# More first-half products before the second half is ready: fifteen tiles instead of ten between output projection and feed-forward

## The chip, the cores and the metric

The kernel runs on one core of one Trainium2 chip. The metric is the device time of one execution in microseconds (us), the median of several runs. The engines are TensorE (PE, with its weight loads PEld), VectorE (DVE), ScalarE (ACT), GpSimd (POOL) and SyncE (SP), which only issues transfers here.

## The reference, cut to what matters

One transformer layer over 640 tokens (128 context, 512 latent) of width 2048. The change lies between these lines:

```
o = concatenate([a, cm, pm], axis=-1) @ w_out
x = x + g1 * rmsnorm(o, g_post_mix)
h = rmsnorm(x, g_pre_ffn) * (1 + sc2) + sh2
gt, up = split(h @ w_ffn_in, 2, axis=-1)       # 2048 x 11264
f = (silu(gt) * up) @ w_ffn_out
x = x + g2 * rmsnorm(f, g_post_ffn)
```

`rmsnorm(x, g)` is `x * rsqrt(mean(x*x) + 1e-6) * g`, the mean being over the 2048 channels of a token.

## The kernel before

Everything is kept transposed: channels on the 128 partitions, tokens along the free dimension, and the 640 tokens are worked on as two halves of 320. Every fp32 operand of a product is split into a high and a low part (`hl`, `X`, `act`), and a product is three matmuls of 128x128 weights on 128x320 tokens (high-high, high-low, low-high, lines 1165 to 1167).

**Output projection.** It runs in two passes, one for each token half. While pass two runs, `chain()` normalises the first half: post-norm, residual, pre-norm, modulation, and the split into `X[1]` and `X[2]`. So when pass two ends, the first half is ready for the feed-forward, and the second is not.

**Feed-forward, first matrix.** There are 44 tiles (`FT`). For each, a 2x2 scheme with seven products (`PROD`, j = 0 to 6) replaces eight. Each product is two granules (z = 0, 1) of 12 matmuls: 14 granules in a tile, 616 in all, 7392 matmuls. Products j = 0 and j = 4 need `X[1]` and `X[2]` alone, that is the first token half; the other five need combinations with the second half (`X[3]` to `X[7]`). For the first `NEARLY` = 10 tiles ("early tiles") products 0 and 4 are done ahead, while the second half is still being normalised; their results `p1` and `f1` are put into DRAM (`ed`) and fetched again by `load_early` when the tile gets its other five products (10 granules, order 1, 2, 3, 6, 5). Tiles 10 to 43 follow, with all seven ("full tiles").

**The stream.** `Stream` S3 issues the granules in a fixed order. `S3.step()` fetches weights (SP queue, five buffers `ra` of 512 KB), splits the granule that is three ahead (`prep`: ACT writes the high part, line 1121, DVE the low part, line 1122), makes the weight sums five ahead (`make`: POOL, lines 1147 and 1150; j = 3 on DVE), issues 12 matmuls into a PSUM bank, and then the evacuations `after()` of the granule before. All engines take their instructions in the order of issue.

**The transition.** `chain2()` does the second half's post-norm and residual, and sums the squares for the pre-norm: DVE multiplies by the norm factor (line 992) and adds x (line 993), ACT squares (line 1001), POOL adds the eight squares into one (line 1004), TensorE sums over partitions with a matrix of ones (line 1009). `prep_steps()` multiplies by the second factor `y2` (line 1320), modulates (ACT, line 1325), forms the combinations of both halves (POOL and DVE, line 1147) and splits them into `X[3]` to `X[7]` (lines 1153 and 1154). Both are generators: between their steps the lists `FILB`, `FILL` and `FILP` say how many S3 steps are issued, 1 + 12 + 29 = 42 granules by the end of the preparation. After that comes the rest of the stream, and with it `mod5()`, the last modulation vector, computed on DVE (lines 1388 and 1390) in one small step after every third granule.

**Memory.** Eight PSUM banks of tag `u` rotate among the products. `p1` and `f1` have four buffers each (`NPF`).

## Time and profile before

| what | value |
|---|---|
| median of 3 runs | 2737.97 us (2735.94 to 2738.11) |
| the profiled execution | 2736.24 us, span 2734.5 us |
| TensorE busy | 2611.9 us (96%) of the span |
| VectorE busy | 2027.8 us (74%) |
| ScalarE, GpSimd busy | 1192.6 us (44%), 681.9 us (25%) |
| end of the output projection's matmuls | about 979.2 us from the start of the span |
| first matmul of the feed-forward's second matrix | 2124.89 us |

The span runs from the first to the last instruction of the profiled execution. All times in the rows are microseconds from its start; a busy TensorE is counted by its matmul records, which overlap. "PEclk" is the granted TensorE clock as a share of 2.4 GHz.

### The profile page before, as it was taken

The page shows a single profiled execution, that of the slowest core. Times are in us where ns is not written, and L with a number is a line of the kernel's source. Part 1 is how long each engine was busy: PE and PEld are TensorE (multiplying, and loading weights), DVE is VectorE, ACT ScalarE, POOL GpSimd, SP SyncE. Part 2 cuts the span into 40 slices and gives each one's busy share as a digit, 9 for nine tenths or more (in the row PEclk, how much of TensorE's full clock was granted, in tenths as well). Part 3 has the DMA queues.
Part 4 walks back from the last instruction along what each step waited for, and adds up shares of the span by engine and source line. Part 5 has one row for each costly group of instructions (what it writes and reads, how often), then busy time and mean ns, then how long its engine had stood idle before and what let it go on. Part 6 is the DMA issues. An engine that isn't in the chain of part 4 may idle for free.

```text
span 2734.5 us, 48244 instructions
## 1 busy us (share of the span) xinstructions
PE 2611.9 (96%) x18874; PEld 2515.4 (92%) x18874; DVE 2027.8 (74%) x3248; ACT 1192.6 (44%) x2427; POOL 681.9 (25%) x572
## 2 busy tenths in 40 slices
PE   5999999999899988999999999999999899999996
PEld 4898998899899987999999999999999899999985
DVE  5558874443545779777888888888786899999966
ACT  4232333333554646333333333333333655555554
POOL 2300020000112435544333333333333111111112
PEclk9999999999999999999999999999999999999998
DMA  8856565653445774443333333333332433333343
GB/s 310 297 187 220 197 195 199 221 189 123 159 147 168 212 250 145 147 160 125 128 107 120 124 117 111 127 125 107 121 124 81 140 107 121 110 120 106 98 130 109
DMA packets 182708, 415.88 MB, mean 152 GB/s; under 512 B 17872, under 2 KB 99920, under 8 KB 181968
## 3 DMA queue, kind: packets, MB, share of 16 engines
q1 hardware_dynamic: 151568, 316.58, 35.2%
q10 hardware_dynamic: 27296, 82.33, 9.5%
q0 software_dynamic: 3616, 13.90, 1.4%
q8 instruction: 148, 2.42, 0.4%
q14 instruction: 80, 0.66, 0.1%
HBM read 373.01 MB, written 39.71 MB: 151 GB/s over the span
## 4 chain that ended last, share of the span: by engine, by line
PE 66%; DVE 17%; ACT 5%; issue 5%; DMA 3%; POOL 2%; ACTq 1%; SPq 0%; DVEq 0%; POOLq 0%
PE pj L310 7%; PE pj L311 7%; PE pj L312 7%; PE u L1167 7%; PE u L1165 7%; PE u L1166 7%; DVE hl L1122 5%; PE bb L1165 3%; PE bb L1167 3%; PE bb L1166 3%; ACT hl L1121 2%; DVE f L1390 2%; PE bc L1165 2%; PE bc L1167 2%; PE bc L1166 2%
## 5 line engine op out<-in xcount | busy, mean ns | idle before, releaser
L1167 PE MATMUL u<-X,hl 128*128 128x320 f32 x2464 | 767.6, 312 | 23.7 <-DVE hl L1122 23.4
L1165 PE MATMUL u<-X,hl 128*128 128x320 f32 x2464 | 767.6, 312 | 8.2 <-ACT hl L1121 4.5
L1166 PE MATMUL u<-X,hl 128*128 128x320 f32 x2464 | 762.8, 310 | 0.0
L310 PE MATMUL pj<-act,hl 128*128 128x320 f32 x1664 | 525.1, 316 | 8.8 <-ACT act L250 4.7
L311 PE MATMUL pj<-act,hl 128*128 128x320 f32 x1664 | 516.0, 310 | 1.2 <-DVE act L150 0.7
L312 PE MATMUL pj<-act,hl 128*128 128x320 f32 x1664 | 515.4, 310 | 0.0
L1167 PEld LDWEIGHTS u<-X,hl 128*128 128x128 f32 x2464 | 464.2, 188 | 34.7 <-DVE hl L1122 34.5
L1165 PEld LDWEIGHTS u<-X,hl 128*128 128x128 f32 x2464 | 464.2, 188 | 15.8 <-ACT hl L1121 8.1
L1166 PEld LDWEIGHTS u<-X,hl 128*128 128x128 f32 x2464 | 464.3, 188 | 0.3 <-issue 0.2
L310 PEld LDWEIGHTS pj<-act,hl 128*128 128x128 f32 x1664 | 314.1, 189 | 33.8 <-issue 15.7
L150 DVE TENSOR_TENSOR hl<-ra,hl 128x512 fp32r<-128x512 f32 x244 | 183.5, 766 | 191.8 <-ACT hl L149 191.3
L311 PEld LDWEIGHTS pj<-act,hl 128*128 128x128 f32 x1664 | 314.2, 189 | 3.5 <-DVE act L150 2.1
L312 PEld LDWEIGHTS pj<-act,hl 128*128 128x128 f32 x1664 | 314.2, 189 | 0.2 <-DVE hl L150 0.2
L1122 DVE TENSOR_TENSOR hl<-ra,hl 128x512 fp32r<-128x512 f32 x264 | 244.0, 933 | 43.0 <-ACT hl L1121 42.5
L1150 POOL TENSOR_TENSOR s<-ra 128x512 f32<-128x512 f32 x88 | 145.0, 1647 | 335.0 <-DMA ra<-in_wfi 116.9
L1121 ACT ACTIVATE hl<-ra 128x512 fp32r<-128x512 f32 x264 | 159.4, 625 | 132.0 <-PE u L1167 106.0
L1121 ACT ACTIVATE hl<-s 128x512 fp32r<-128x512 f32 x176 | 110.2, 626 | 236.7 <-DVE s L1147 197.3
L1122 DVE TENSOR_TENSOR hl<-s,hl 128x512 fp32r<-128x512 f32 x176 | 133.4, 762 | 82.0 <-ACT hl L1121 80.9
L149 ACT ACTIVATE hl<-ra 128x512 fp32r<-128x512 f32 x244 | 148.2, 631 | 100.8 <-PE pj L312 56.9
L1122 DVE TENSOR_TENSOR hl<-sy,hl 128x512 fp32r<-128x512 f32 x176 | 139.2, 791 | 67.6 <-ACT hl L1121 67.2
L1147 POOL TENSOR_TENSOR sy<-ra,sy 128x512 f32<-128x512 f32 x88 | 133.7, 1519 | 151.4 <-DVE hl L1122 151.4
L1150 POOL TENSOR_TENSOR T<-T,raw 128x384 f32<-128x384 f32 (+1 forms) x56 | 54.8, 979 | 457.2 <-DVE T L1150 438.0
(343 smaller groups left out, 4926.3 us busy)
## 6 DMA issues: line engine op xcount, KB each, us to landing
ra<-in_wfi SPq DMA_DIRECT2D x196, 512.0 KB, 4.2
rb<-in_wada SPq DMA_DIRECT2D x96, 512.0 KB, 5.5
ra<-in_wada SPq DMA_DIRECT2D x64, 512.0 KB, 6.2
ra<-in_win ACTq DMA_DIRECT2D x56, 512.0 KB, 4.8
ra<-in_wout ACTq DMA_DIRECT2D x56, 512.0 KB, 4.1
raw<-in_wfo SPq DMA_DIRECT2D x48, 576.0 KB, 4.0
f<-in_wada SPq DMA_DIRECT2D x128, 128.0 KB, 2.1
fd<-f ACTq DMA_DIRECT2D x44, 320.0 KB, 2.2
```

Source lines behind the costliest of these rows:

```text
L149: act_e.activation(h, src, AF.Copy)
L150: dve.tensor_tensor(out=l, in0=src, in1=h.bitcast(F32), op=ALU.subtract)
L310: pe.matmul(ps, w[:, 0, k, :], rhs_h, start=start, stop=False)
L311: pe.matmul(ps, w[:, 0, k, :], rhs_l, start=False, stop=False)
L312: pe.matmul(ps, w[:, 1, k, :], rhs_h, start=False, stop=stop)
L1121: act_e.activation(g.hl[:, 0, :n], src, AF.Copy)
L1122: dve.tensor_tensor(out=g.hl[:, 1, :n], in0=src, in1=g.hl[:, 0, :n].bitcast(F32), op=ALU.subtract)
L1147: e.tensor_tensor(out=out, in0=a, in1=b, op=ALU.subtract)
L1150: e.tensor_tensor(out=out, in0=a, in1=b, op=ALU.add)
L1165: pe.matmul(ps, w[:, 0, j, :], xh, start=first and j == 0, stop=False, skip_group_check=True)
L1166: pe.matmul(ps, w[:, 0, j, :], xl, start=False, stop=False, skip_group_check=True)
L1167: pe.matmul(ps, w[:, 1, j, :], xh, start=False, stop=stop and j == n - 1, skip_group_check=True)
```

## The change

The early tiles become 15. `FILL` and `FILP` are rewritten (with `FILB` 1 + 18 + 44 = 63 granules by the end of the preparation). The tiles are then taken in the order 0, 15, 1, 16, ... 14, 29 and 30 to 43 (`ORDER3`), so an early tile alternates with a full one, and `mod5()` begins at once, a step after every fourth granule as long as early tiles are in the order, then after every third. In `chain2()` the squares are summed by TensorE alone: sixteen matmuls with the matrix of ones in place of seven POOL additions and two matmuls; DVE takes over the one block (i = 5) that POOL had. Both norm factors are written to PSUM banks (tags `y`, `s`), and six banks stay for `u`. The eight POOL subtractions for `X[7]` are issued between the splits in place of ahead of them. The weights of the feed-forward's first granules are fetched and split earlier, while the last output tile is projected. `p1` keeps three buffers and `f1` two; `mod5()` gets tiles of its own.

```
-        P2["y2"] = yst.enter_context(tc.tile_pool(name="yp", ...)).tile([P, TH], F32, tag="y2", name="y2")
...
-    def rsqrt_half(ps, y):
+    def rsqrt_half(ps, y, out=None):
...
-        rsqrt_to(y, v, t, ps[:, :TH], 1.0 / D)
-        return y
+        rsqrt_to(y, v, t, ps[:, :TH], 1.0 / D, out)
+        return y if out is None else out
...
-        y = rsqrt_half(ps, y_tile()).unsqueeze(1).to_broadcast([P, 2, TH])
+        y = rsqrt_half(ps, y_tile(), bank3("y", "y")).unsqueeze(1).to_broadcast([P, 2, TH])
         yield
         sq = {}
+        ps = bank3("xss", "s")
         for i in range(KP + 3):
             if i < KP:
-                e, t = (pool if i == 5 else dve), X["b", i]
-                e.tensor_tensor(out=t, in0=t, in1=y, op=ALU.mult)
-                e.tensor_tensor(out=t, in0=t, in1=x[i], op=ALU.add)
+                t = X["b", i]
+                dve.tensor_tensor(out=t, in0=t, in1=y, op=ALU.mult)
+                dve.tensor_tensor(out=t, in0=t, in1=x[i], op=ALU.add)
...
-            if k > 0:
-                pool.tensor_tensor(out=sq[0], in0=sq[0], in1=sq[k], op=ALU.add)
+            if k >= 0:
+                for z in range(2):
+                    pe.matmul(ps, ones, sq[k][:, z, :], start=k == 0 and z == 0, stop=k == KP - 1 and z == 1)
                 drop(sq[k])
             yield
-        ps = bank3("xss")
-        for z in range(2):
-            pe.matmul(ps, ones, sq[0][:, z, :], start=z == 0, stop=z == 1)
-        drop(sq[0])
-        rsqrt_half(ps, P2["y2"])
+        P2["y2"] = rsqrt_half(ps, y_tile(), bank3("y2", "y"))
...
-            if hf and n == KT - 1 and g == 1:
+            if hf and (n, g) == (KT - 2, 3):
                 x_item(lambda: S3.fetch())
+            if hf and (n, g) == (KT - 1, 2):
+                x_item(lambda: S3.prep(2))
...
-    def bank3(name="u"):
-        return P3["ps"].tile([P, 512], F32, tag="u", name=name)[:, :TH]
+    def bank3(name="u", tag="u"):
+        return P3["ps"].tile([P, 512], F32, tag=tag, bufs=6 if tag == "u" else 1, name=name)[:, :TH]
...
-    NEARLY, NPF = 10, 4
+    NEARLY, NPF = 15, {"p1": 3, "f1": 2}
-    FILB, FILL = 1, (1, 1, 1, 1, 1, 1, 2, 1, 1, 1, 0, 1)
-    FILP = (2, 2, 1, 1, 1, 1, 1, 1, 1, 1, 1, 1, 2, 3, 2, 2, 2, 2, 1, 3)
+    FILB, FILL = 1, (1, 2, 2, 2, 1, 2, 2, 2, 1, 1, 1, 1)
+    FILP = (1, 1, 2, 2, 3, 2, 3, 2, 2, 2, 2, 1, 3, 3, 4, 3, 2, 2, 2, 2)
+    ORDER3 = [i for e in range(NEARLY) for i in (e, NEARLY + e)] + list(range(2 * NEARLY, FT))
...
-            load_early(i + 1)
+            n = ORDER3.index(i) + 1
+            if n < FT:
+                load_early(ORDER3[n])
...
-        for k in range(KP):
-            sub(pool, ov(1, k), ov(1, KP + k), ov(1, k))
...
+                if src is hb and k % 2:
+                    n = KP // 2 * h + k // 2
+                    sub(pool, ov(1, n), ov(1, KP + n), ov(1, n))
...
-    for i in range(FT):
+    for i in ORDER3:
...
-    while S3.i < n_early + 10 * NEARLY + 2:
-        S3.step()
     bg = mod5()
     while S3.step():
-        if S3.i % 3 == 0:
+        if S3.i % (4 if S3.i < n_early + 24 * NEARLY else 3) == 0:
             next(bg, None)
```

## Rows read from the trace of the kernel before

**Rows 1.** The page: busy time of each engine, share, instructions.

```profile
PE 2611.9 (96%) x18874; PEld 2515.4 (92%) x18874; DVE 2027.8 (74%) x3248; ACT 1192.6 (44%) x2427; POOL 681.9 (25%) x572
```

**Rows 2.** Windows: busy us (instructions) by engine, clock, DMA share, GB/s.

```profile
1000.00:1010.00 10.00, 7.04 (x37) 6.64 (x38) 9.96 (x9) 4.50 (x8) 6.61 (x4) 0.83 1.06 389
1050.00:1060.00 10.00, 6.08 (x36) 5.29 (x36) 10.00 (x12) 6.39 (x15) 8.82 (x8) 1.00 0.33 111
...
979.20:1021.50 42.30, 32.41 (x183) 29.42 (x182) 36.33 (x40) 18.07 (x33) 17.84 (x10) 0.92 0.87 297
1021.50:1055.10 33.60, 26.27 (x165) 23.89 (x163) 33.52 (x43) 22.48 (x46) 21.81 (x19) 1.00 0.45 133
1055.10:1088.60 33.50, 28.45 (x178) 27.66 (x178) 32.45 (x52) 18.89 (x44) 17.38 (x12) 0.95 0.50 152
1126.00:1300.00 174.00, 170.76 (x1135) 166.24 (x1134) 133.45 (x184) 64.90 (x117) 82.22 (x54) 1.00 0.45 143
```

**Rows 3.** Windows, the feed-forward's matmuls (tile u) alone.

```profile
979.20:1126.00 146.80, 121.85 (x756) 0.97 0.59 188
...
1300.00:2125.00 825.00, 816.38 (x5505) 1.00 0.35 117
```

**Rows 4.** Timeline of TensorE: start, us, instruction.

```profile
986.33 0.31 PE L1167 MATMUL u<-X,hl 128*128 128x320 f32 x1
...
992.78 0.31 PE L1166 MATMUL u<-X,hl 128*128 128x320 f32 x1
...
1017.56 1.34 PE L1009 MATMUL xss<-sq,ones 128*128 128x320 f32 x4 [0.28 <-POOL sq L1004]
...
1018.89 0.31 PE L1166 MATMUL u<-X,hl 128*128 128x320 f32 x1
```

**Rows 5.** Waits of TensorE, 960 to 1250 us, and of VectorE, 979 to 1126 us: total, times, longest.

```profile
PE u L1167 <- DVE hl L1122: 20.7, 25, 3.5
...
DVE hl L1122 <- ACT hl L1121: 15.6, 12, 8.1
```

**Rows 6.** By source line or tile: duration ns min/median/max, first and last start.

```profile
L993 DVE TENSOR_TENSOR ob<-ob,x x7: 824/2036/2082, 989.3 to 1012.8; 128x640 f32<-128x640 f32 x7
L1320 DVE TENSOR_TENSOR ob<-ob,y x8: 812/1296/1504, 1021.5 to 1041.2; 128x640 f32<-128x640 f32 x8
L1150 DVE TENSOR_TENSOR f<-u,p x21: 475/482/484, 997.6 to 1277.8; 128x320 f32<-128x320 f32 x21
```

**Rows 7.** Groups by line and shape, 979 to 1092 us: busy, mean ns.

```profile
L1122 DVE TENSOR_TENSOR hl<-ra,hl 128x512 fp32r<-128x512 f32 x40 | 38.6, 985 | 9.1 <-ACT hl L1121 9.0
L1320 DVE TENSOR_TENSOR ob<-ob,y 128x640 f32<-128x640 f32 x8 | 9.8, 1227 | 0.0
L993 DVE TENSOR_TENSOR ob<-ob,x 128x640 f32<-128x640 f32 x7 | 10.7, 1531 | 0.2
L992 DVE TENSOR_TENSOR ob<-ob,rs_y 128x640 f32<-128x640 f32 x7 | 7.7, 1093 | 0.0
```

**Rows 8.** Timelines of GpSimd and VectorE.

```profile
1006.19 3.69 POOL L1004 TENSOR_TENSOR sq<-sq,sq 128x640 f32<-128x640 f32 x2 [1.59 <-ACT sq L1001]
...
1008.37 0.48 DVE L1150 TENSOR_TENSOR f<-u,p 128x320 f32<-128x320 f32 x1
...
1028.90 0.48 DVE L1147 TENSOR_TENSOR t<-ob,hb 128x320 f32<-128x320 f32 x1
1029.43 0.69 DVE L1122 TENSOR_TENSOR hl<-ra,hl 128x512 fp32r<-128x512 f32 x1
...
1036.46 1.35 DVE L1122 TENSOR_TENSOR hl<-ra,hl 128x512 fp32r<-128x512 f32 x1
```

**Rows 9.** Groups by line and shape, 1131 to 1260 us (early tiles): waits for ACT.

```profile
L1122 DVE TENSOR_TENSOR hl<-sy,hl 128x512 fp32r<-128x512 f32 x28 | 29.2, 1042 | 5.5 <-ACT hl L1121 5.5
L1122 DVE TENSOR_TENSOR hl<-s,hl 128x512 fp32r<-128x512 f32 x27 | 18.6, 689 | 18.2 <-ACT hl L1121 18.2
```

**Rows 10.** Groups by line and shape, 1400 to 1800 us: a step of `mod5()`.

```profile
L1390 DVE SCALAR_TENSOR_TENSOR f<-f,vec,f 128x256 f32<-128x256 f32 x124 | 69.8, 603 | 0.0
```

More of the change, by code (lines that the diff above doesn't have):

```diff
@@ L851, in trunk_kernel @@
     XR = ExitStack()
-    yst = ExitStack()
     stb = ExitStack()
@@ L873, in begin_pass2 @@
             X["b", k] = slot_tile(f"ob{k}")
-        P2["y2"] = yst.enter_context(tc.tile_pool(name="yp", bufs=1, side="right")).tile([P, TH], F32, tag="y2", name="y2")
         P3["e"] = eps.enter_context(tc.tile_pool(name="ep3", bufs=1, side="right", reuse_waits="tile"))
@@ L1231, in in_unit, with w3t @@
         S3.grans += grans
-    def w3t(tag, bufs=1):
-        return P3["e" if bufs > 1 else "p"].tile([P, TH], F32, tag=tag, bufs=bufs, name=tag)
+    def w3t(tag):
+        return P3["e" if tag in NPF else "p"].tile([P, TH], F32, tag=tag, bufs=NPF.get(tag, 1), name=tag)
     def load_early(i):
@@ L1238, in load_early @@
             for z, n in enumerate(("p1", "f1")):
-                t = early_st[i][n] = w3t(n, NPF)
+                t = early_st[i][n] = w3t(n)
                 sp.dma_start(out=t, in_=ed[i, z])
@@ L1245, in after @@
         if j == 0:
-            st["p1"] = w3t("p1", NPF)
+            st["p1"] = w3t("p1")
             act_e.activation(st["p1"], st["a"], AF.Copy)
@@ L1257, in after @@
             add(dve, st["u3"], st["b"], st["u3"])
-            load_early(i + 1)
+            n = ORDER3.index(i) + 1
+            if n < FT:
+                load_early(ORDER3[n])
         elif j == 4 and early_:
-            st["f1"] = w3t("f1", NPF)
+            st["f1"] = w3t("f1")
             add(dve, st["f1"], st["e"], st["p1"])
@@ L1289, in trunk_kernel @@
     early.close()
-    P3["ps"] = pst.enter_context(tc.tile_pool(name="ps3", bufs=8, space=PSUM))
+    P3["ps"] = pst.enter_context(tc.tile_pool(name="ps3", bufs=1, space=PSUM))
     P3["p"] = x37.enter_context(tc.tile_pool(name="tp3", bufs=1, reuse_waits="tile"))
@@ L1371, in mod5 @@
         sc, bias, gains = vec[:, :2 * KT], vec[:, 2 * KT:3 * KT], vec[:, 3 * KT:]
-        acc, raw = ([w3t("f1", NPF) for _ in range(2)] for _ in range(2))
+        acc, raw = ([P3["e"].tile([P, 256 if i else TH], F32, tag=f"m5{n}{i}", name=f"m5{n}{i}") for i in range(2)] for n in "ar")
         def load(i):
@@ L1417, in trunk_kernel @@
     eps.close()
-    yst.close()
     XR.close()
```

## The prediction

> **What bounds the kernel now.** I read the page first. TensorE is busy for 96% of the span [rows 1], so the bound is TensorE's own work, and a gain can only come from where it stands still. The windows of 10 us across the change's place show where: from 990 to 1060 us TensorE's busy time falls to 6 or 7 of 10 us while VectorE's is 10 of 10, and in one of these windows the granted clock averages 0.83 of 2.4 GHz [rows 2]. The waits name the partner: of TensorE's waits between 960 and 1250 us, 20.7 us are for the low part of a weight split, made by VectorE [rows 5].
>
> Busy time hides slow and missing matmuls, so I count. At full clock 44 matmuls start between 986.33 and 992.78 us, 0.1466 us each [rows 4]; a granule of 12 takes 1.76 us. The projection's last matmul stands at about 979.2 us. From there to 1126.0 us there are 756 feed-forward matmuls, exactly 63 granules, in 146.8 us [rows 3]. Their own time is 756 x 0.1466 = 110.8 us. So some 36 us of TensorE pass in the transition without a feed-forward matmul. The new lists issue 63 granules by the end of the preparation, so this is the stretch to compare. The rest has less to give: 1135 matmuls in 174.0 us of mostly early tiles (7.6 us over their own time) [rows 2], 5505 in 825 us of mostly full ones (18 us) [rows 3].
>
> **More early granules.** The number of granules, 616, stays. Their work in the transition becomes 63 granules in place of 43 or so, without new TensorE work. What they need there is VectorE: 15 more splits in the preparation and 6 more in `chain2`.
>
> **The squares on TensorE.** The four records of two fp32 matmuls and one ordinary matmul take 1018.89 - 1017.56 = 1.33 us [rows 4]; less 0.15 that is 0.59 us for one with the matrix of ones. Fourteen more cost 14 x 0.59 = 8.3 us of TensorE, which stand in its queue between granules and are not hidden. With the first sum there are 17, 10.0 us.
>
> **POOL out of `chain2`.** Seven additions go. What they cost is seen on VectorE: while POOL adds squares, the residual addition takes 2.04 to 2.08 us, and 0.82 without it [rows 6]; a split takes 1.35 us beside POOL and 0.69 alone [rows 8]. `chain2` with the stall before it is the window 979.2 to 1021.5 us, VectorE busy 36.3 us [rows 2]. Changes: the seven residual additions from 10.7 to 8 x 0.82 = 6.6 us, the multiplications from 7.7 to 6.6 [rows 7], splits freed of POOL about -3.7 (five or six of the thirteen, 0.66 us each), six more splits 6 x 0.69 = +4.1, another evacuation or two at 0.48, +0.7: 32.2 us. TensorE needs 19 x 1.76 + 10.0 = 43.4 us there. So `chain2` turns from VectorE's to TensorE's stage.
>
> **The factors in PSUM.** An addition with one operand in PSUM took 475 to 484 ns in all 21 cases, one of them (1008.37 us) in the middle of POOL's work, whereas operations with both operands in SBUF double [rows 6, 8]. So I price the eight multiplications by `y2` at 0.82 us each, 6.6 us for 9.8 [rows 7], a gain of 3.2. Bounds: 0 (the contention goes on to the next instruction instead) and 3.2. [...]
>
> **The preparation.** Its two windows last 67.1 us, VectorE busy 66.0 [rows 2]. Changes: -3.2; 15 more splits at 0.69 to 0.985 us (the mean of this stretch [rows 7]), +10.4 to +14.8, I take 12.5, since POOL's subtractions are the same in number and are only spread out; four more evacuations, +1.9. Sum 77.2 us. TensorE needs 44 x 1.76 = 77.4 us. The two are equal, which matters for what is left over. ScalarE has 41.4 us of work in these windows [rows 2] and 15 x 0.63 more: not the bound.
>
> **Fetch and split ahead of the end of the projection.** It takes away TensorE's pause at 979 us and the fall towards the lower clock level, 1.2 GHz, behind it (mean 0.92 from 979.2 to 1021.5 us [rows 2]); both are in the 36 us. On SP's queue the first weight fetches now stand ahead of the last writes of the first half's result, which is read only in the middle of `chain2`; I see nobody who waits, and price it at nothing. If a weight buffer came free late, the queue would hold these writes for as long, under 5 us.
>
> **Transfers.** Six more granules in `chain2` want 6 x 256 KB = 1.5 MB where the DMA engines are full (389 GB/s [rows 2]), 4 us of them. The stage grows to 43 us without other new transfers but the results of one or two early tiles, so this is covered; without cover it is 4 us. Two buffers for `f1` are enough as long as its write lands within two tiles, 14 us at the new rate.
>
> **Sum for the transition.** At best 63 x 1.76 + 10.0 = 120.9 us against 146.8: 25.9 us gained, the added matmuls included. What stays as stall: with VectorE and TensorE equal, a wait of VectorE on ScalarE comes through. It waited 15.6 us in all, 8.1 of them at one place, the longest, ahead of the first split, which goes [rows 5]; I leave the other 7.5 in and round to 8. Bounds: 0 (three granules of lead cover all) and 24 (the 44 splits of the preparation as slow as those beside POOL: 44 x (1.35 - 0.985) = 16 more).
>
> **The mixed order.** After granule 63 the same granules remain, but more of them in early tiles. An early tile loses about 0.8 us (7.6 us over 94.6 granules), a full one 0.55 (18 us over 458.8 granules, with `mod5`). About seven more early tiles and five fewer full ones: 7 x 0.8 - 5 x 0.55 = +2.9 us if each keeps its loss; I take 3. Bounds: -4 (a full tile between two early ones gives VectorE time to catch up, so that early tiles lose no more than full ones) and +45 (below).
>
> **Forecast.** 25.9 - 8 - 3 = 14.9 us less than the profiled execution's 2736.24 us, 2721.3; the median of the runs shown is 1.7 us higher than that execution, so 2723 us, 0.5% faster.
>
> **Rivals.**
> (a) VectorE stays the bound in the preparation. For it: 100% busy now, and 15 splits more. Against it: `chain2` no longer spends VectorE. With 18 to 20 us left as stall the gain is 3 to 5 us: 2734 us, inside the 0.2% (5.5 us) that a measurement can tell from no change.
> (b) Slower: `mod5` in the mixed order. In the early tiles VectorE is busy 76.7% [rows 2], and waits on ScalarE for splits another 23.7 us of 129 (18%) [rows 9]: nearly full by dependences. A step of `mod5` is two operations of 0.60 us [rows 10], 1.2 us; an early tile gets 2.5 of them, 3.0 us. If TensorE waits for all that, 15 x 3.0 = 45 us, 2738 - 17.9 + 45 = 2765 us with the gain of the transition. Against it: the full tile behind it gets 3.5 steps for 4.7, and three granules of lead bridge 5 us. It decides at about 1.2 us for each pair (17.9 us / 15): there the gain is gone.
> (c) More: all 25.9 us and the relief of the mixed order, 30 us: 2708 us.
>
> **Chances.** Forecast, 2714 to 2731 us: 0.57. (a) 0.17, (b) 0.14, with times from 2733 up to 2765, (c) 0.12. Faster by over 0.2%, below 2732.5: the forecast, (c) and a small part of (a), 0.72. Within 0.2%: most of (a), a third of (b), 0.17. Slower: 0.11. The range leaves out the lowest of (c) and the worse part of (b): 2706 to 2739.
>
> **What would show it.** In the new trace, the 756th feed-forward matmul some 128.9 us after the projection's last one, 18 us earlier than now; no clock below 1.00 between 980 and 1020 us; the multiplications of lines 992 and 1320 all near 0.82 us, POOL idle in `chain2`; sixteen more fp32 matmuls at 0.59 us; VectorE still at 95% or more in the preparation, with TensorE's waits there under 8 us in total. Then, in the mixed order, TensorE within 1% of the pace of now. The prediction is wrong if the residual additions stay at 2 us without POOL (then something else doubles them), if the preparation lasts over 90 us, or if waits for line 1122 recur in each early tile by over 1 us.

## The result

The changed kernel takes 2757.38 us (median of 6 runs, 2755.43 to 2762.97) where the kernel before takes 2738.04 us beside it: 0.7% slower, ratio 1.007 with the interval [1.0059, 1.008]. Forecast were 2723 us, in a range of 2706 to 2739 us.

Line numbers of the changed kernel are up to two lower around the stream and up to four higher in `mod5()` (the matmuls are lines 1163 to 1165, ScalarE's and VectorE's parts of a split 1119 and 1120, the additions of `after()` 1148, the `mod5` step 1392 and 1394, its load 1380, a weight fetch 1091).

**The transition after.** First the page's busy times of the changed kernel, beside [rows 1]:

```profile
PE 2621.6 (95%) x18902; PEld 2516.4 (91%) x18902; DVE 2021.4 (73%) x3255; ACT 1187.6 (43%) x2427; POOL 652.4 (24%) x563
```

TensorE is busy 9.7 us longer, fourteen more products with the matrix of ones included, and its share fell: it stands still longer. The windows by engine of the changed kernel (busy us and instructions of PE, PEld, DVE, ACT, POOL, then the clock, the DMA share, GB/s), beside [rows 2], say that this is not in the transition:

```profile
981.30:1021.50 40.20, 39.73 (x245) 37.21 (x246) 28.58 (x43) 18.65 (x34) 0.88 (x1) 1.00 0.99 344
1021.50:1055.00 33.50, 33.50 (x227) 33.18 (x227) 30.82 (x45) 23.60 (x47) 15.48 (x14) 1.00 0.57 168
1055.00:1090.00 35.00, 33.37 (x227) 33.11 (x227) 31.18 (x48) 20.20 (x45) 13.31 (x12) 1.00 0.66 198
...
1000.00:1010.00 10.00, 10.00 (x61) 9.18 (x60) 7.50 (x12) 4.43 (x8) 0.00 (x0) 1.00 1.06 384
1050.00:1060.00 10.00, 10.00 (x70) 10.00 (x70) 9.97 (x15) 5.95 (x13) 5.91 (x6) 1.00 0.70 215
```

In the last two rows TensorE is busy 10.00 of 10 us where it had 7.04 and 6.08, the granted clock stays at 1.00 where it averaged 0.83 in the first of them, and VectorE is down from 36.3 to 28.6 us in `chain2()`. That is GpSimd's absence: with the squares on GpSimd again (e7 below) VectorE is busy 36.5 us in the same part, 980.2 to 1021.5 us. Of TensorE's waits from 960 to 1110 us 4.2 us are left, the largest row of them below. In the same stretch the kernel before waits 23.3 us, 19.5 of them for the low parts of splits ([rows 5] count these to 1250 us):

```profile
PE u L1165 <- DVE hl L1120: 2.1, 3, 1.6
```

The durations of VectorE's multiplication by the first factor, of the residual addition, and of the multiplication by `y2` (source lines, ns min/median/max, first and last start) answer to [rows 6]. All three are at the undisturbed 0.81 to 0.83 us; the addition was at 2.04:

```profile
L991 DVE TENSOR_TENSOR ob<-ob,y x8: 810/812/816, 987.5 to 1010.3; 128x640 f32<-128x640 f32 x8
...
L992 DVE TENSOR_TENSOR ob<-ob,x x8: 824/825/826, 988.3 to 1011.2; 128x640 f32<-128x640 f32 x8
...
L1323 DVE TENSOR_TENSOR ob<-ob,y x8: 804/808/820, 1025.7 to 1048.6; 128x640 f32<-128x640 f32 x8
```

**Where the time went.** The most useful view of this study counts work done, not busy time. Windows of the feed-forward's matmuls alone (tile `u`), cut where matmul 756 (the end of the transition, 63 granules), matmul 5040 (granule 420, the end of the changed kernel's mixed order) and matmul 7392 (the last) are reached. A first window starts half a microsecond ahead of the first matmul. A count can be a few over or under, since the cuts are rounded. First the kernel before, then the changed one:

```profile
980.40:1125.90 145.50, 121.75 (x756) 0.96 0.59 189
1125.90:1773.35 647.45, 638.74 (x4286) 1.00 0.38 126
1773.35:2123.95 350.60, 348.24 (x2355) 1.00 0.34 114
```

```profile
981.30:1104.35 123.05, 115.18 (x756) 1.00 0.72 231
1104.35:1789.90 685.55, 649.93 (x4286) 1.00 0.39 129
1789.90:2142.40 352.50, 349.07 (x2355) 1.00 0.34 114
```

The transition is 22.5 us shorter. The second stretch, with the same number of matmuls and nearly as many `mod5` steps (93 in the kernel before, 90 in the changed one), is 38.1 us longer, the third 1.9 us. That leaves +17.5 us; the stretches ahead and behind add 1.6, and the spans (2753.6 and 2734.5 us) differ by 19.1. So the gain was there and was lost nearly twice over, behind the transition. TensorE's waits of 1105 to 1760 us name three partners:

```profile
PE u L1163 <- DVE f L1148: 14.1, 15, 1.3
PE u L1163 <- ACT hl L1119: 10.8, 15, 0.9
PE u L1165 <- DVE hl L1120: 7.2, 30, 0.4
```

Fifteen, fifteen and thirty times, for fifteen pairs of one early and one full tile. The waits stand at one place of each pair, the third to the sixth granule of the early tile, but for eight of the thirty, which stand in the full tile. The largest, for VectorE's addition of line 1148 into `f`, is an early tile's product j = 3, which accumulates into the bank that j = 1 left and so must wait until VectorE has read it.

### The profile page after: what moved, and what is told of

It is laid out like the page before. It is cut to its first block, busy times and chain, and to the rows that moved or that the text cites. A ratio compares the mean times of both kernels' runs of the same rounds, so it can differ in the third digit from the quotient of the medians.

```text
span 2753.6 us, 48339 instructions
## 1 busy us (share of the span) xinstructions
PE 2621.6 (95%) x18902; PEld 2516.4 (91%) x18902; DVE 2021.4 (73%) x3255; ACT 1187.6 (43%) x2427; POOL 652.4 (24%) x563
## 4 chain that ended last, share of the span: by engine, by line
PE 63%; DVE 17%; DMA 6%; ACT 5%; issue 5%; POOL 2%; SPq 1%; ACTq 1%; DVEq 0%; POOLq 0%
PE pj L310 8%; PE pj L311 7%; PE pj L312 7%; PE u L1165 6%; PE u L1163 6%; DVE hl L1120 6%; PE u L1164 5%; DMA ra<-in_wfi 3%; PE bb L1163 3%; ACT hl L1119 3%; DVE m5a L1394 3%; PE bb L1165 3%; PE bb L1164 3%; PE bc L1163 2%; PE bc L1165 2%
## 5 line engine op out<-in xcount | busy, mean ns | idle before, releaser
L1119 ACT ACTIVATE hl<-sy 128x512 fp32r<-128x512 f32 x176 | 108.9, 627 | 188.4 <-PE u L1165 92.7
L1145 POOL TENSOR_TENSOR sy<-s,ra 128x512 f32<-128x512 f32 x88 | 125.3, 1424 | 204.2 <-DMA ra<-in_wfi 184.5
```

What stands on the lines that cost most here:

```text
L1119: act_e.activation(g.hl[:, 0, :n], src, AF.Copy)
L1145: e.tensor_tensor(out=out, in0=a, in1=b, op=ALU.subtract)
```

## The experiments

I call the 24 granules of a pair (ten of the early tile, then fourteen of the full one) by the number issued in it: a `mod5` step at place 0 comes just ahead of the early tile's first granule. Three theories could explain the 38.1 us. **A**: the `mod5` steps hold VectorE in a stretch with no slack (A1: by their time, wherever they stand; A2: only near the early tile). **B**: a `mod5` load that waits for its buffer stands in SyncE's queue and holds the weight fetches behind it. **C**: the alternation of tiles by itself.

All runs in one table: the places of the steps in each pair, the buffers for their loads, the two stretches between the marks, the whole (median, or the one run where there is no interval) and its ratio to the kernel before. The stretches are those of one profiled execution, which can stand some 5 us off the median (e3's span is 2726.8 us).

| kernel | places in a pair | buffers | 756 to 5040 | 5040 to 7392 | whole, us | ratio, interval |
|---|---|---|---|---|---|---|
| before | early tiles first | 2 | 647.4 | 350.6 | 2738.04 | |
| after | 0 4 8 12 16 20 | 2 | 685.6 | 352.5 | 2757.38 | 1.007 [1.0059, 1.008] |
| e1 | none | 2 | 634.0 | 405.5 | 2754.7 | one run |
| e2 | 0 4 8 12 16 20 | 3 | 688.8 | 347.2 | 2749.15 | 1.004 [1.0025, 1.0055] |
| e3 | early tiles first | 2 | 653.5 | 358.9 | 2731.25 | 0.9976 [0.9964, 0.9989] |
| e4 | early tiles first | 3 | 650.1 | 350.6 | 2714.14 | 0.9909 [0.9893, 0.9926] |
| e5 | 11 14 17 20 23 | 2 | 660.6 | 359.9 | 2739.19 | 1.0005 [0.9995, 1.0014] |
| e6 | 4 12 20 | 2 | 651.4 | 372.2 | 2742.81 | one run |
| e7 | as e3 | 2 | 660.3 | 358.8 | 2735.16 | 0.9987 [0.9977, 0.9997] |
| e8 | as e3 | 2 | 659.7 | 359.5 | 2735.64 | 0.9987 [0.9977, 0.9997] |
| e9 | early tiles first | 2 | 658.8 | 358.9 | 2742.48 | 1.001 [1.0, 1.002] |
| e10 | as after, half the work | 2 | 682.0 | 347.1 | 2747.86 | one run |
| e12 | 11 14 17 20 23 | 3 | 646.0 | 349.8 | 2713.6 | 0.9903 [0.9888, 0.9918] |
| e13 | as before | 3 | 638.0 | 346.7 | 2727.37 | 0.9958 [0.9941, 0.9974] |
| e14 | 2 4 6 8 9 | 3 | 663.7 | 350.5 | 2729.11 | one run |
| e15 | 10 12 14 17 20 22 | 3 | 660.1 | 350.2 | 2729.16 | 0.9968 [0.9956, 0.9979] |
| e17 | 2 6 10 14 18 22 | 3 | 670.8 | 347.2 | 2731.86 | 0.9979 [0.9969, 0.9989] |
| e18 | 0 8 16 | 2 | 674.3 | 370.6 | 2766.01 | one run |
| e19 | as e2, later end of tile | 3 | 652.5 | 348.2 | 2717.39 | 0.9927 [0.9912, 0.9942] |
| e20 | as e12, later end of tile | 3 | 632.5 | 351.1 | 2700.28 | 0.9866 [0.985, 0.9882] |

### Is it the order, the steps, or the queue?

**e1_mod5_late**: the changed kernel without a `mod5` step as long as early tiles are in the order.

```
-        if S3.i % (4 if S3.i < n_early + 24 * NEARLY else 3) == 0:
+        if S3.i >= n_early + 24 * NEARLY and S3.i % 4:
```

> The changed kernel, but no step of mod5 while early tiles are in the order; after granule 420 it gets three steps in four granules. What is read is the stretch from the 756th to the 5040th feed-forward matmul (granules 63 to 420, own time 628 us): 680 us in the changed kernel, 644 us in the kernel before. Theory A (mod5's own VectorE time, 3.0 us in each early tile, makes the splits late): 640 to 648 us. Theory B (mod5's loads stand on SP's queue until VectorE has read the buffer, and the weight fetches behind them come late): also 640 to 648 us. Theory C (the alternation itself: where an early tile follows a full one or the reverse, weight buffers and sums come free too late, with mod5 or without): 665 to 680 us. The whole time says nothing, since mod5 is crowded into the last 196 granules and VectorE is over-full there: it may be 2750 to 2800 us.

The second window of the feed-forward's matmuls (756 to 5040):

```profile
1101.35:1735.35 634.00, 632.04 (x4286) 1.00 0.39 123
```

634.0 us: 13 us less than the kernel before needs with its steps, and 6 us over the matmuls' own time (4284 x 0.1466 = 628.0 us), so the alternation by itself costs 6 us at the most. C falls; the steps cost 51.6 us here, 3.4 us for each pair. Put into the third stretch, three behind every four granules, they lengthen that by 53 us, so there is no room for all of them there either.

**e2_mod5_three_buffers**: three buffers for the loads of `mod5`.

```
-                sp.dma_start(out=raw[i % 2][:, :256], in_=wada2[i // KT, i % KT])
+                sp.dma_start(out=raw[i % 3][:, :256], in_=wada2[i // KT, i % KT])
```

> The changed kernel, but mod5's weights have three buffers in place of two, so that a load goes into a buffer that VectorE read a whole step earlier, and SP's queue need not wait for VectorE. VectorE's work is the same. Theory B: SP's waits for mod5's operations (411 us in the mixed order) all but vanish, the stretch from matmul 756 to 5040 falls from 680 to 645 to 660 us, and the time to 2722 to 2740 us. Theory A: SP's waits vanish, the stretch and the time stay (676 to 684 us, 2753 to 2761 us). Theory C: the same as A, or a gain under 8 us.

SyncE's waits ahead of its transfers from 1110 to 1750 us (line 1380 is the `mod5` load), in the changed kernel and in e2:

```profile
SPq L1380 <- DVE m5a L1394: 348.6, 69, 11.3
```

```profile
SPq L1380 <- DVE m5a L1394: 16.2, 9, 2.0
```

The wait that B speaks of is gone, and the stretch is as long as before, 688.8 us. So B alone isn't the cause of this loss; what the third buffer does at the bad place is read further down. The third stretch gains 5.3 us (352.5 to 347.2), and the whole is less slow, 1.004 for 1.007.

**e3_early_tiles_first** and **e4_first_and_three**: the changed kernel in the old order of tiles, with two and with three buffers.

```
-    ORDER3 = [i for e in range(NEARLY) for i in (e, NEARLY + e)] + list(range(2 * NEARLY, FT))
+    ORDER3 = list(range(FT))
...
-        if S3.i % (4 if S3.i < n_early + 24 * NEARLY else 3) == 0:
+        if S3.i > n_early + 10 * NEARLY + 2 and S3.i * 3 % 8 < 3:
```

> The changed kernel with the order of tiles of the kernel before: the fifteen early tiles first, then 15 to 43, and mod5 after the early tiles, three steps in eight granules. Transition as changed. All of A, B and C expect it faster than the kernel before: the transition's 21 us stay, less 3 us for five more early tiles: 2716 to 2726 us. If six PSUM banks in place of eight, or three and two buffers for p1 and f1, were the cause (theory D), it stays above 2740 us.

> The kernel of early tiles first, and mod5 with three buffers. Theory B: the full tiles with mod5 lose less than now (0.55 us each), so 5 to 12 us below the run with early tiles first alone: 2708 to 2718 us. Theories A and C: within 3 us of that run.

e3 takes 2731.25 us: without the mixed order the change is 0.24% faster than the kernel before. It doesn't keep its 22 us: the two stretches are 14 us longer than before's. The likely reason, which no run separates, is that fifteen early tiles leave fewer granules for the steps, which come denser (three behind eight granules). e4 keeps them: 2714.14 us, 0.9% faster than the kernel before. So B's queue does cost time where the early tiles come first.

**e13_before_three_buffers**: the same third buffer in the kernel before (and three buffers in place of four for `p1`, to make room).

> The kernel before, with three buffers for the mod5 loads instead of two (and three instead of four for the early tiles' p1, to make room). If three buffers alone are what e4_first_and_three won over e3_early_tiles_first, it is won here as well: 2721 to 2730 us. If before's waits of SyncE for these buffers (463 us in 116 waits) stand beside a TensorE that has all it needs (its stretches 647.4 and 350.6 us are already no longer than those of e4), the time stays at 2733 to 2739 us, and what e4 gains over before is the transition's 22 us.

2727.37 us, 0.42% faster; its stretches fall from 647.4 and 350.6 to 638.0 and 346.7 us. The kernel before lost some 11 us in SyncE's queue, with a TensorE that seemed to have all it needs. The same buffer is worth 17 us from e3 to e4, so a good part of e4's 24 us is not the transition's.

### What of the transition's edits gives the gain?

**e9_granules_alone**: the kernel before with fifteen early tiles, the new lists and three steps behind eight granules, nothing else.

```
-    NEARLY, NPF = 10, 4
+    NEARLY, NPF = 15, 4
...
-        if S3.i % 3 == 0:
+        if S3.i * 3 % 8 < 3:
```

> The kernel before with fifteen early tiles and the new lists FILL and FILP alone (mod5 after the early tiles, three steps in eight granules); squares by GpSimd, factors in SBUF, eight PSUM banks, no early fetch. Read from the first feed-forward matmul to the 756th: 145 us before, 122.5 us in the changed kernel. The prediction's account: VectorE stays the bound of both stages, with 21 more splits at 0.7 to 1.0 us in them: 124 to 135 us, so that most of the 22 us come from the granules alone and the other edits give 2 to 12 us. The rival: without the other edits VectorE is over-full and nothing is gained, 138 us or more.

The transition takes 126.0 us: 19 of the 22.5 us come from the lists of granules alone. The whole stays where it was, 2742.48 us; as in e3, longer stretches behind it (658.8 and 358.9 us) give the gain back. This kernel has eight banks and four buffers for `p1` and `f1`, so e3's fewer banks and buffers are not needed to explain its longer stretches.

**e7_squares_by_pool**: e3 with GpSimd adding the squares again.

```
-            if k >= 0:
-                for z in range(2):
-                    pe.matmul(ps, ones, sq[k][:, z, :], start=k == 0 and z == 0, stop=k == KP - 1 and z == 1)
+            if k > 0:
+                pool.tensor_tensor(out=sq[0], in0=sq[0], in1=sq[k], op=ALU.add)
```

> The kernel with the early tiles first, but the squares are added by GpSimd again (seven additions) and TensorE has two matmuls with the matrix of ones; VectorE keeps the block i = 5. Read from the first feed-forward matmul to the 756th, 123 us with the squares on TensorE. The prediction's account: TensorE has 8.3 us less to do in chain2, but VectorE's operations double beside GpSimd, some 9 us more, and chain2 becomes VectorE's stage again: 122 to 130 us, whole time within 6 us of the run with early tiles first. A rival: TensorE's 8.3 us weigh more than the contention, and it is faster: 114 to 118 us.

**e8_y2_in_sbuf**: e3 with the second norm factor in SBUF.

```
-        P2["y2"] = rsqrt_half(ps, y_tile(), bank3("y2", "y"))
+        P2["y2"] = rsqrt_half(ps, P3["e"].tile([P, TH], F32, tag="m5a0", name="y2"))
```

> The norm factor y2 goes to an SBUF tile instead of a PSUM bank; everything else as in e3_early_tiles_first. If a factor in PSUM is what keeps VectorE's products free of GpSimd's reads (as the rows of 1.35 and 2.04 us against 0.69 and 0.82 us for operations with both inputs in SBUF would have it), the transition (matmul 1 to 756 of the feed-forward) grows by up to 4 us over 123.0 us and the whole to 2731 to 2736 us. If the place of the factor makes no difference here, because TensorE never waits for these products any more, the transition stays at 122 to 124 us and the whole at 2729 to 2733 us. [...]

The transitions: 123.0 us in e3, 122.4 in e7, 125.2 in e8. Where the squares are added makes no difference that these runs can tell: with GpSimd adding, TensorE is spared 14 products with ones and waits 5.8 us for VectorE's low parts where it waits 2.1 in e3. For the factor's place the multiplication itself shows little, first e3, then e8 (source line 1323):

```profile
L1323 DVE TENSOR_TENSOR ob<-ob,y x8: 803/810/821, 1023.7 to 1046.6; 128x640 f32<-128x640 f32 x8
```

```profile
L1323 DVE TENSOR_TENSOR ob<-ob,y x8: 810/816/1108, 1023.5 to 1047.2; 128x640 f32<-128x640 f32 x8
```

With the factor in SBUF two of the eight (1.11 and 1.09 us) are slowed beside GpSimd, with the factor in PSUM none. In e7, too, the eight multiplications by the first factor, which lies in PSUM, stay at 804 to 815 ns while GpSimd adds squares, and the residual additions, with both operands in SBUF, reach 1925 ns. For the transition it is worth some 2 us in these two executions, and the wholes of e3 and e8 can't be told apart (their intervals overlap). No cost of a factor in PSUM shows in these rows: their median is 810 ns with it there (e3) and 816 ns with it in SBUF (e8).

### Number, work or place of the steps?

**e5_mod5_in_full_tiles**: five steps for each pair, all behind granules of the full tile; **e6_mod5_every_eighth**: three, behind every eighth granule. (The third stretch gets three behind eight and one behind two.)

```
-        if S3.i % (4 if S3.i < n_early + 24 * NEARLY else 3) == 0:
+        if (S3.i - n_early) % 24 in (11, 14, 17, 20, 23) if S3.i < n_early + 24 * NEARLY else S3.i * 3 % 8 < 3:
...
+        if S3.i % (8 if S3.i < n_early + 24 * NEARLY else 2) == 0:
```

> The changed kernel (alternating order), but in each pair of tiles mod5 gets five steps, all behind granules of the full tile, none behind those of the early tile; then three steps in eight granules. From matmul 756 to 5040 the changed kernel took 686 us, and 633 without any step there. Theory A1 (VectorE's total over a pair of tiles is too much): the loss goes with the number of steps, 5 for 6, so 672 to 680 us. Theory A2 (the place counts: a step among the splits of the early tile, whose chain of ScalarE and VectorE has no slack, is what TensorE waits for): 635 to 650 us, and the whole kernel at 2710 to 2725 us.

> The changed kernel with mod5 at half the dose while early tiles are in the order: a step after every eighth granule, then after every second. Read from matmul 756 to 5040. A1 (total of VectorE): half the loss or less, 640 to 660 us. A2 (place): the steps stand at three fixed places in a pair of 24 granules, of which one or two are behind granules of the early tile in place of two or three: 645 to 665 us. The run tells only how the loss grows with the dose; after matmul 5040 it may be slower than the changed kernel's 352 us, up to 375.

Over e1, five steps in the full tile cost 26.6 us, three cost 17.4, six cost 51.6. Not by number alone, then; e5 lies between what A1 and A2 would have.

**e10_half_steps**: the changed kernel with half of VectorE's work in a step; it leaves out half of the modulation's products.

```
-                for c in range(2):
+                for c in range(1 if kt else 2):
```

> The changed kernel, with its order, but in each mod5 step after the first of a group VectorE does one of its two operations (the second 128 outputs keep only the first of the products: half of the modulation's products are left out). The steps, their loads and their places stay. If it is VectorE's time that the steps take out of the mixed stretch (the three-part wait f, hl, hl of TensorE), the stretch from matmul 756 to 5040 falls from 685.6 us towards that of a half dose: 650 to 665 us, and the whole to about 2722 to 2737 us. If each step costs a fixed sum whatever VectorE does in it (its loads in the queue, its place in the order of instructions), the stretch stays at 675 to 690 us.

682.0 us for 685.6: no more than one execution can differ from another. It looks as if VectorE's time were not what is short, but the rows further down show that this run hardly shortened it where it counts; it doesn't decide about A1.

**e12_full_and_three**: e5 with three buffers.

> e5_mod5_in_full_tiles (mod5 steps only behind granules of full tiles) with three buffers for the mod5 loads instead of two. If the loss of e5 over e1 came of SyncE's queue, which stands still while a load waits for its buffer, the stretch from matmul 756 to 5040 falls from 660.6 to 645 to 655 us and the whole to 2722 to 2730 us. If it is VectorE's time alone, the stretch stays at 658 to 662 us, and only what follows gains some 5 to 10 us, as in e2 and e4: the whole is 2729 to 2735 us.

646.0 us in the stretch, and 349.8 behind it: here the queue did matter, 14.6 us of it, and the whole is 2713.6 us, 8 us below what the queue's theory had. So B is at work in the mixed order too, and the same buffer that gains 14.6 us here gains nothing in e2.

Where does e2 lose? Its matmuls, cut at single granules, show one place in each pair: granules 2 and 3 of the early tile take 6.6 us (3.5 us of their own), all others 3.5 to 4.2 for two. Below are windows of the feed-forward's matmuls around the pair that starts at 1326.5 us, and the three matmuls of the timeline at which TensorE stood still:

```profile
1326.55:1330.05 3.50, 3.50 (x26) 1.00 0.16 18
1330.05:1336.75 6.70, 4.13 (x25) 1.00 0.36 139
```

```profile
1332.41 0.42 PE L1163 MATMUL u<-X,hl 128*128 128x320 f32 x1 [0.52 <-ACT hl L1119]
...
1333.14 0.41 PE L1165 MATMUL u<-X,hl 128*128 128x320 f32 x1 [0.17 <-DVE hl L1120]
...
1336.80 0.38 PE L1163 MATMUL u<-X,hl 128*128 128x320 f32 x1 [1.93 <-DVE f L1148]
```

VectorE, ScalarE and GpSimd of e2 in the same microseconds:

```profile
1327.04 1.92 DVE L1394 SCALAR_TENSOR_TENSOR m5a<-m5r,vec,m5a 128x256 f32<-128x256 f32 x2
1328.88 0.68 DVE L1120 TENSOR_TENSOR hl<-s,hl 128x512 fp32r<-128x512 f32 x1
1329.48 0.48 DVE L1148 TENSOR_TENSOR f<-u,f 128x320 f32<-128x320 f32 x1
1330.50 0.49 DVE L1279 TENSOR_TENSOR f<-f,u 128x320 f32<-128x320 f32 x1 [0.54 <-ACT f L1278]
1332.39 0.69 DVE L1120 TENSOR_TENSOR hl<-s,hl 128x512 fp32r<-128x512 f32 x1 [1.40 <-ACT hl L1119]
1333.00 1.78 DVE L1145 TENSOR_TENSOR s<-ra 128x512 f32<-128x512 f32 x1
1335.56 0.69 DVE L1120 TENSOR_TENSOR hl<-s,hl 128x512 fp32r<-128x512 f32 x1 [0.78 <-ACT hl L1119]
1336.17 0.48 DVE L1148 TENSOR_TENSOR f<-u,p 128x320 f32<-128x320 f32 x1
```

```profile
1329.99 0.47 ACT L1278 ACTIVATE f<-f 128x320 f32<-128x320 f32 x1 [3.74 <-DVE f L1148]
1331.02 0.33 ACTq L1281 DMA_DIRECT2D fd<-f  x1
1331.73 0.63 ACT L1119 ACTIVATE hl<-s 128x512 fp32r<-128x512 f32 x1 [1.26 <-DVE f L1279]
```

```profile
1327.20 1.48 POOL L1145 TENSOR_TENSOR sy<-ra,sy 128x512 f32<-128x512 f32 x1 [0.63 <-DVE hl L1120]
1332.51 1.73 POOL L1148 TENSOR_TENSOR s<-ra 128x512 f32<-128x512 f32 x1 [3.83 <-DMA ra<-in_wfi]
```

Read from the top. The step at place 0 (1.92 us, beside GpSimd) stands ahead of the full tile's last addition (1329.48). ScalarE, in order, has been idle 3.74 us ahead of the Silu of that sum; VectorE waits 0.54 us for the Silu to multiply by it; ScalarE waits for that product, which ends at 1330.99, before it issues the tile's store at 1331.02, and 1.26 us pass between its Silu and its next split, the early tile's. Then come VectorE's low part, 1.40 us late, the next addition into `f`, and TensorE's 1.93 us. So a tile's end passes three times between two engines, and the next tile's splits stand behind it in ScalarE's order.

These rows also show where e2 gives back what its third buffer may save. VectorE's subtraction of line 1145 (1333.00) takes 1.78 us, since GpSimd's addition began 0.5 us ahead of it; in the changed kernel VectorE begins first (1334.90, GpSimd at 1335.13) and it takes 0.68 us. Both durations are the same in all fourteen pairs with a step at place 0. From the step's start to the next addition into `f` e2 needs 9.1 us, the changed kernel 8.3 (1328.94 to 1337.21): 0.8 us of each pair are lost at the seam.

And they tell why e10 helped so little. Its VectorE at the same place:

```profile
1326.61 0.47 DVE L1394 SCALAR_TENSOR_TENSOR m5a<-m5r,vec,m5a 128x256 f32<-128x256 f32 x1
1327.01 1.78 DVE L1120 TENSOR_TENSOR hl<-s,hl 128x512 fp32r<-128x512 f32 x1
1328.71 0.48 DVE L1148 TENSOR_TENSOR f<-u,f 128x320 f32<-128x320 f32 x1
```

The step is down to 0.47 us, but the split behind it now stands beside GpSimd's addition (1326.76 to 1328.23) and takes 1.78 us in place of 0.68. The full tile's last addition comes 2.10 us behind the step's start, where it came 2.45 us behind it in the changed kernel (1328.94 to 1331.39), and so in all fourteen pairs.

**e18_other_eighths**, **e17_steps_two_later**, **e14_early_but_the_first** and **e15_six_in_full_tiles** move the steps. e18 is e6 with `S3.i % 8 == 4`; e17 is e2 with `S3.i % 4 == 2`; e14 and e15 are e12 with other places (the table has them).

> e6_mod5_every_eighth with its three mod5 steps of each pair of tiles moved by four granules: the places 0, 8 and 16 of 24, not 4, 12 and 20; two buffers, as there. If the number of steps decides, the stretch from matmul 756 to 5040 takes 648 to 656 us, as in e6 (651.4 us). If the step at place 0 does, it takes 665 to 685 us.

> e2_mod5_three_buffers with every mod5 step of the mixed stretch two granules later: the places 2, 6, 10, 14, 18 and 22 of each pair of tiles, not 0, 4, 8, 12, 16 and 20. Nothing else differs. If the step at place 0, the start of an early tile, is what holds TensorE for 3.1 us in each pair (45 us in 15 pairs), the stretch from matmul 756 to 5040 falls from 688.8 to 640 to 655 us and the whole to 2705 to 2720 us. If the number of steps or their work decides, it stays at 680 to 690 us, and the whole at 2742 to 2752 us.

> e12_full_and_three, with its five mod5 steps of each pair of tiles behind granules of the early tile, but none at the pair's start: at the places 2, 4, 6, 8 and 9 of 24, not 11, 14, 17, 20 and 23. If any step near an early tile costs much (its ten granules ask more of VectorE than those of a full tile), the stretch from matmul 756 to 5040 grows from 646.0 us to 665 to 690 us. If it is the step at the pair's start alone, where the last sums of a full tile, ScalarE's Silu and the first splits of the early tile wait for each other, the stretch is 644 to 655 us.

> e12_full_and_three with six mod5 steps in each pair of tiles, not five, all behind granules of the full tile (places 10, 12, 14, 17, 20 and 22 of 24). That is as many as in e2_mod5_three_buffers, whose stretch from matmul 756 to 5040 took 688.8 us. If their number decides, it takes 675 to 690 us again. If their place decides, it takes 646 to 655 us and the whole 2705 to 2716 us.

Windows of the feed-forward's matmuls, 756 to 5040, and TensorE's largest wait for the addition into `f` from 1105 to 1750 us. First e6:

```profile
1102.90:1754.30 651.40, 641.29 (x4286) 1.00 0.39 128
```

```profile
PE u L1163 <- DVE f L1148: 1.2, 2, 0.8
```

Then e18:

```profile
1102.50:1776.80 674.30, 642.55 (x4286) 1.00 0.38 123
```

```profile
PE u L1163 <- DVE f L1148: 18.0, 15, 1.7
```

As many steps, moved by four granules: 22.9 us more, and the wait is there in each of the 15 pairs (the first pair's, 0.8 us, is in every run of the mixed order, e1 included). The place decides over the number. The other three fell between what I had expected: e17 loses 18.0 us less than e2, not the 34 to 49 us that place 0 alone would give. Its step at place 2 stands ahead of the early tile's first addition into `f`, the other end of the same chain. e14 and e15 come out at 663.7 and 660.1 us, so a step at another place isn't free: over e1, five around the early tile cost 29.7 us, six mostly behind the full one 26.1, and e12's five 12.0. What each of these other places costs was not separated.

### Taking the tile's end out of the way

**e19_tile_end_later** is e2, with a full tile's Silu, product and store one product later in the order of the instructions. **e20_best_tile_end_later** is e12 with the same.

```
             add(dve, f2, st["c"], f2)
-            act_e.activation(f2, f2, AF.Silu)
-            dve.tensor_tensor(out=f2, in0=f2, in1=st["u3"], op=ALU.mult)
-        if j == (5 if i < NEARLY else 6):
+            def end():
+                act_e.activation(f2, f2, AF.Silu)
+                dve.tensor_tensor(out=f2, in0=f2, in1=st["u3"], op=ALU.mult)
+                if i >= NEARLY:
+                    act_e.dma_start(out=fd[i], in_=st["f"])
+            if i < NEARLY or i == ORDER3[-1]:
+                end()
+            else:
+                ends.append(end)
+        if ends and j != 6:
+            ends.pop()()
+        if j == 5 and i < NEARLY:
             act_e.dma_start(out=fd[i], in_=st["f"])
```

> e2_mod5_three_buffers (mixed order, six steps at the places 0, 4, 8, 12, 16 and 20, three buffers), but the last part of a full tile (ScalarE's Silu, VectorE's product with it, and the store that ScalarE issues) comes one product later in the order of the instructions, behind the first sum of the next tile. If the step at place 0 costs so much because this end stands between the step and the next splits (the step delays VectorE's last sum, ScalarE waits for the sum with its Silu and for the product with its store, and the early tile's splits stand behind both), TensorE's stall of 3.1 us in each pair falls to about 1 us: the stretch from matmul 756 to 5040 falls from 688.8 to 645 to 665 us and the whole to 2715 to 2730 us. If the end of the tile is no link (VectorE's own order is), the stretch stays at 680 to 692 us.

> e12_full_and_three with the same later end of each full tile. If the end of the tile is the link, the 12 us that its mixed stretch still loses (646.0 against 634.0 us without a step) fall to some 4 us, and the whole to 2700 to 2710 us, the fastest of all. If not, the stretch stays at 644 to 649 us and the whole at 2711 to 2717 us.

Windows, 756 to 5040, of e19 and then of e20:

```profile
1105.35:1757.80 652.45, 641.52 (x4286) 1.00 0.42 136
```

```profile
1104.25:1736.80 632.55, 630.37 (x4287) 1.00 0.42 137
```

With all six steps at the very places of e2, the stretch falls by 36.3 us. VectorE is busy 556.6 us in it, against 563.1 in e2's 688.8 us and 532.8 in the changed kernel's 685.6: it was not the sum of its work that was too large, so A1 falls. VectorE and ScalarE of e19 at the same kind of place (a pair's start):

```profile
1319.28 1.92 DVE L1406 SCALAR_TENSOR_TENSOR m5a<-m5r,vec,m5a 128x256 f32<-128x256 f32 x2
...
1321.72 0.48 DVE L1148 TENSOR_TENSOR f<-u,f 128x320 f32<-128x320 f32 x1
...
1324.79 0.48 DVE L1148 TENSOR_TENSOR f<-u,p 128x320 f32<-128x320 f32 x1
1325.19 1.18 DVE L1283 TENSOR_TENSOR f<-f,u 128x320 f32<-128x320 f32 x1
```

```profile
1318.88 0.64 ACT L1119 ACTIVATE hl<-s 128x512 fp32r<-128x512 f32 x1 [0.40 <-PE u L1165]
1323.51 0.63 ACT L1119 ACTIVATE hl<-s 128x512 fp32r<-128x512 f32 x1 [3.99 <-DVE s L1145]
...
1324.41 0.46 ACT L1282 ACTIVATE f<-f 128x320 f32<-128x320 f32 x1
```

The step is as long, 1.92 us. But the next addition into `f` comes 5.5 us behind the step's start (1319.28 to 1324.79), where it came 9.1 us behind it in e2 (1327.04 to 1336.17), because ScalarE's split of 1318.88 no longer stands behind a Silu, and the Silu (1324.41) finds its sum ready. Of the 3.6 us between them 1.1 are VectorE's subtraction of line 1145, which now comes ahead of GpSimd's addition and takes 0.68 us (1322.72) in place of 1.78. Of the 24.3 us that TensorE waited for that addition in e2 (1105 to 1750 us) 0.8 are left. The edit takes the product out of VectorE's order as well as the Silu and the store out of ScalarE's; which of the three counts most was not separated. e20 takes 2700.28 us, 1.34% faster than the kernel before, and its stretch is as short as e1's without any step.

## Why the prediction was wrong

The terms, in the prediction's order:

- **The transition** was right, and better than its sum. From the projection's last matmul to the 756th of the feed-forward it takes 123.8 us (forecast 128.9, at best 120.9): the stall left is 3 us, where I took 8. The preparation was to be VectorE's and TensorE's in equal parts; it is TensorE's, VectorE is busy 92% and 89% of its two windows, and TensorE's waits are 4 us. The clock, the 0.82 us operations and the idle GpSimd came as said: the clock is 1.00 in every microsecond from 981 to 1021 us, where the kernel before has 0.50 from 983 to 986 us and from 1004 to 1006 us (the traces give a share of full speed, none in GHz). TensorE's pause behind the projection did not go, but fell from 1.5 to 0.9 us. One reading was too even: between 1010 and 1040 us TensorE had been busy 8.0, 9.7 and 7.9 of 10 us, not 6 or 7; no term rests on it.
- **The squares and the factors** were priced about right as single terms (0.81 us for each multiplication, as said, and 0.54 us for each product with ones, for 0.59: 996.51 to 997.88 us holds two of them and two ordinary matmuls), but they decide little: e9 gets 19 of the 22.5 us without either, e7 and e8 keep the transition within 1 and 2.3 us of e3's. The gain was in the granules.
- **The mixed order** is the step that failed: "+2.9 us if each keeps its loss; I take 3". The loss of a tile isn't carried with it; it depends on what stands beside it. It measured +40.0 us (38.1 and 1.9). Rival (b) had its place and its size (45 us, 2765 us), and the prediction gave it 0.14.
- **Rival (b)'s mechanism** was half right. Its cause, `mod5` in the mixed order, is shown by e1. Its price, all of VectorE's time in an early tile's 2.5 steps, is not what is paid: three steps moved by four granules differ by 22.9 us (e18 against e6), and with the full tile's end moved out of the way the same six steps cost 36.3 us less (e19 against e2). What I missed in reading the trace of before was the order inside ScalarE at the seam of two tiles. The sentence against it, that three granules of lead bridge 5 us, failed there: the lead is in splits, and the splits themselves stood behind the seam. Nor did the sign that it named come, waits for the low part of over 1 us in each early tile: that row has 7.2 us in 30 waits of 0.4 at the most, and the loss shows under the addition into `f` and ScalarE's high part.

In the kernel before, the steps begin when the early tiles are done, and no early tile follows a full one; so neither [rows 9] nor [rows 10] could show the seam with a step in it. It could have been found by writing down, for one seam, the instructions of each engine in program order.

**Open.** What the other places of a step cost one by one isn't known, and e19 moves three parts of a tile's end at once. Half steps with three buffers were not run, nor was the later end of a tile tried in the kernel before.

## What to carry to other kernels

Count finished work between fixed marks of two traces before explaining anything: it showed at once that the edit worked and that its gain was lost behind it. When the order of work changes, price the seams and not the pieces: for each new neighbourhood write down what each in-order engine has queued, and let no engine that must prepare the next piece wait inside the end of the last one. And background work is placed, not only rationed: three steps in the wrong places cost more than five in the right ones, and one more load buffer was worth 11 us in a kernel whose waiting queue looked harmless.

## What the runs showed of the hardware that was not expected

A transfer that waited for its buffer held the one behind it in the same engine's queue: in the changed kernel SyncE stood 9.3 us ahead of the `mod5` load of 1330.89 us, until VectorE's step on that buffer ended at 1330.86, and issued the weight fetch behind it at 1331.31. TensorE's waits name no transfer, in the kernel before 8.3 us from 1126 to 2124 us, all for VectorE and ScalarE. Yet SyncE waited 348.6 us for `mod5` buffers in the changed kernel's mixed stretch; to take that wait away gained nothing there (e2), but 14.6 us with the steps at other places (e5 against e12) and 11 us in the kernel before (e13). ScalarE also stood still ahead of a transfer that it issues itself, until its data was there: at one seam of e2 0.56 us (1330.46 to 1331.02), with the next split behind it. A VectorE operation with both operands in SBUF that began beside a running GpSimd addition took 1.78 us in place of 0.68 (e2's subtraction of 1333.00 us, e10's split of 1327.01), so time cut out of one operation came back in the next one (e10). And a VectorE multiplication with its factor in PSUM took 810 ns at the median (e3), with both operands in SBUF 816 ns (e8): the place of the operand cost nothing here but beside GpSimd, where the SBUF form took up to 1.11 us.
